# Modulation rows of a two-layer diffusion backbone: turned by VectorE and folded by one matmul, gate row by rounded parts, one section's row sums on VectorE

## The chip, the core and the metric

The kernel runs on one core of a Trainium2 chip. The core has a matmul engine (TensorE, PE in the profile, with its weight loads shown apart as PEld), VectorE (DVE), ScalarE (ACT), GpSimd (POOL) and SyncE (SP), which here only issues DMA transfers. Each engine works through its own list of instructions in order and waits on semaphores for the others. The metric is device time in microseconds (us); several runs are given by their median.

## What is computed

Two transformer layers over 512 latent tokens and 256 context tokens of width 1024. Layer 0 mixes tokens by differential attention (8 heads), layer 1 by grouped-query attention. What the change touches is the adaptive normalisation: for each layer a conditioning vector is multiplied with a 1024 x 3072 matrix, once for the latent tokens (`c`) and once for the context (`c_ctx`), and the result is cut into shift, scale and gate.

```python
def adaln(cvec, w, b):
    m = jax.nn.silu(cvec) @ w + b
    return jnp.split(m, 3, axis=-1)
...
for i in range(DEPTH):
    last = i == DEPTH - 1
    shift, scale, gate = adaln(c, ada_w[i], ada_b[i])
    ...
    cshift, cscale, cgate = adaln(c_ctx, ada_w[i], ada_b[i])
    h = rms_norm(x, pre_g[i]) * (1.0 + scale) + shift
    hc = rms_norm(xc, pre_g[i]) * (1.0 + cscale) + cshift
    ...
    x = x + gate * rms_norm(y, post_g[i])
    if not last:
        xc = xc + cgate * rms_norm(yc, post_g[i])
return x
```

## The kernel before

All matmuls that must be exact to fp32 are made of three fp32r matmuls: each operand is split into a rounded part (`hi`, a ScalarE cast) and the rest (`lo`, a subtraction on GpSimd or VectorE), and hi·hi, hi·lo and lo·hi are summed in PSUM. A plain fp32 matmul is possible too.

**The order of the work.** The program is first recorded as a list of operations by a planner (`Plan`), which prices every operation, keeps track of data, of buffer rings and of PSUM banks, and draws an order for each engine in several passes; `Emit.chain` then fixes that order on every engine. All instructions therefore carry one line number in the profile (L452, the recorder's `add`), and they are told apart by the names of their tiles. Any change of the recorded operations makes the planner draw every engine's order anew.

**The stages.** At the start the tokens are normalised and turned, and layer 0's shift and scale are computed from 32-row blocks (`cols4`, `ada_red`). Then layer 0's heads 0 to 7 run: for each, projections of q, k, v and the gate path z, scores (`sc`), a softmax on VectorE and ScalarE into `pp`, a turn of `pp` (a 32 x 32 block transpose on VectorE, a write to DRAM as `dr`, a reload as `at`), a split of `at` into `ah` and `al`, and the products with v. PSUM has four banks `bk0` to `bk3` and two double banks `sc`. Then come the output projection, the norms of layer 1 and layer 1's heads.

**The modulation in the background.** While layer 0's heads run, the rest of the modulation is computed piece by piece (`acc_steps`). It has six sections of 512 columns, in the order `SECS`: (0,4) and (0,5) are the two halves of layer 0's gate, (1,0), (1,2), (1,1), (1,3) are layer 1's shift and scale. Each section is two groups of four weight blocks; `grp_load` brings a group by one DMA of 1 MB into the single buffer `araw`, `grp_mm` multiplies it, and the next group's load follows.

In `grp_mm` each of the four blocks j goes to its own 32 rows of one PSUM bank. The stationary operand is `s32[:, k, :]`, 32 columns of which the first two hold silu(c) and silu(c_ctx) for block k and the rest are zero. So row 32j+v of the bank holds the part of block j for vector v. The first group is copied to `arow` by ScalarE, the second is added by VectorE. A section listed in `SUMS` would go another way: VectorE multiplies each weight block with the silu column and adds it up, in one `arow` tile for each vector. `SUMS` is empty.

What remains is to add the four blocks over the partitions:

- `ada1_finish` (layer 1's shift and scale) needs the result in columns, one value for each partition. It runs four fp32 matmuls with a 128 x 128 piece of `arow` as weights and `sel32` (128 x 2, ones at rows 32j+v) as the moving operand; `mod_cols` then adds the bias.
- `gate0_finish` (layer 0's gate) needs the row on all partitions. For each of the two vectors it runs one fp32 matmul whose weight is a column of `sel32` broadcast to 128 columns and whose moving operand is all 512 columns of `arow`. VectorE then adds the bias and multiplies.

`ones` and `ones_r` are 128 x 128 tiles of ones, used to warm PE up and to add over partitions (`colsum`).

Of the kernel before, what the change touches and what calls it, by code (L numbers as in the profile page):

```python
# [8 lines left out]
F32 = mybir.dt.float32  # L9
# [6 lines left out]
P = 128  # L16
# [17 lines left out]
ACD = 5.0  # L34
SUMS = ()
FILL1 = (('z', 0), ('q', 2), ('q', 1), ('z', 2), ('z', 1), ('q', 3), ('z', 3), ('z', 4), ('z', 5), ('z', 7), ('z', 6))
# [53 lines left out]
def f32(ap):  # L90
    return ap.bitcast(F32)
# [447 lines left out]
def tile_backbone(  # L539
# [23 lines left out]
    def nm(s):  # L563
        uid[0] += 1
        return f"{s}_{uid[0]}"
# [83 lines left out]
    def heads_out(dst, o, moved):  # L649
# [7 lines left out]
        out=ident, in_=ident, compare_op=ALU.not_equal, fill=1.0, base=0, pattern=[[-1, P]], channel_multiplier=1)  # L657
    ones = con.tile([P, P], F32, name="ones")
    nc.vector.memset(ones, 1.0)
    ones_r = con.tile([P, P], F32R, name="ones_r")  # L660
    nc.vector.tensor_copy(ones_r, ones)
    eps = con.tile([P, 1], F32, name="eps")
# [305 lines left out]
    cp = pool_c.enter_context(pl.pool("cp", "right"))  # L968
    s32 = cp.tile([P, KT, 32], F32, name="s32", bufs=1)
    nc.vector.memset(s32, 0.0)  # L970
    nc.vector.tensor_copy(s32[:, :, 0:2], scv)
    sel32 = cp.tile([P, 2], F32, name="sel32", bufs=1)
    nc.vector.tensor_reduce(sel32, ident.rearrange("p (j r) -> p r j", j=4)[:, 0:2, :], AX.X, ALU.add)
    selb = [sel32[:, v:v + 1].to_broadcast([P, P]) for v in range(2)]

# [3 lines left out]
    def cols4(o, g, ts):  # L979
        prev = None  # L980
        for j in (3, 2, 1, 0):
            with after(prev):
                prev = nc.tensor.matmul(
                    o[32 * j:32 * j + 32, :], s32[:, 4 * g + j, :], ts[j], start=g == 0, stop=g == 1)

# [242 lines left out]
    with pl.pool("t0") as t0:  # L1228
# [11 lines left out]
        def grp_mm(i):  # L1240
# [13 lines left out]
            else:  # L1254
                o = trp()
                prev = None
                for j in range(4):
                    with after(prev):
                        prev = nc.tensor.matmul(o[32 * j:32 * j + 32, :], s32[:, 4 * g + j, :], t[:, j, :], start=True, stop=True)
                r, = rows[layer, sec]  # L1260
# [6 lines left out]
        def ada1_finish(layer, sec):  # L1267
            r = rows.pop((layer, sec))
            o = trp()
            if (layer, sec) in SUMS:  # L1270
                for b in range(8):
                    v, k = divmod(b, 4)
                    nc.tensor.matmul(o[:, b:b + 1], r[v][:, k * P:(k + 1) * P], ones[:, :1], start=b == 0, stop=b == 7)
                ov_ = o[:, :8].rearrange("p (v k) -> p v k", v=2)
            else:
                for b in range(4):
                    nc.tensor.matmul(o[:, 2 * b:2 * b + 2], r[0][:, b * P:(b + 1) * P], sel32, start=b == 0, stop=b == 3)
                ov_ = o[:, :8].rearrange("p (k v) -> p v k", v=2)
            mod_cols(layer, sec % 2, sec // 2, lambda v: ov_[:, v, :])
# [293 lines left out]
        def gate0_finish(half):  # L1573
            r = rows.pop((0, 4 + half))
            sl = slice(half * 512, half * 512 + 512)
            b = bcast(ada_b[0, 2 * D + half * 512:2 * D + half * 512 + 512])
            g = bcast(post_g[0, sl])
            for v in range(2):
                o = trp()
                nc.tensor.matmul(o, *((ones, r[v]) if (0, 4 + half) in SUMS else (selb[v], r[0])), start=True, stop=True)  # L1580
                nc.vector.tensor_tensor(gate0[v][:, sl], o, b, ALU.add)
                nc.vector.tensor_tensor(gate0[v][:, sl], gate0[v][:, sl], g, ALU.mult)
# [712 lines left out]
```

## Time and profile before

| what | value |
| --- | --- |
| median of 3 runs | 764.67 us (764.32 to 766.8) |
| the profiled execution | 763.36 us |
| its span, first to last instruction | 761.6 us |
| instructions | 14035 |
| mean granted clock of the matmul engine | 0.995 |
| data moved by DMA | 131.77 MB, 173 GB/s in the mean |

The busy times of the engines, the stages and the waits are quoted in the prediction. In the profile a line names engine, operation and tiles (result, arrow, operands), the number of instructions, busy time or mean duration, and behind it the idle time of that engine just before and what ended it. A plain fp32 matmul shows as two records, an fp32r matmul as one. The end of a matmul is modelled, so the step from one start to the next tells what it costs PE, not its duration.

### The profile page before, as it was taken

Reading aid. Unit: us, or ns where it says so; the run is one execution under the profiler, and the core shown is the slowest. Engines: PE = TensorE matmul, PEld = TensorE weight load, DVE = VectorE, ACT = ScalarE, POOL = GpSimd, SP = SyncE. Lnnn points to the kernel's source line nnn. Section 1 sums busy time; section 2 is a strip of 40 time slices with the busy share of each in tenths; the row PEclk is TensorE's granted clock in tenths of the full one; section 3 lists DMA queues with packets and bytes.
Section 4 is the critical chain, followed back from the end, with each engine's and each line's share of the span. In section 5 each row is a group of like instructions: output and inputs, shape, how many; then the busy total and the mean of one; then the engine's idle time right before and its main releaser. Section 6 shows DMA issues by size and latency. Waiting matters only on the chain. (4 is left out here: it accounts for less than half of the span.)

```text
span 761.6 us, 14035 instructions
## 1 busy us (share of the span) xinstructions
PE 741.4 (97%) x5070; PEld 657.9 (86%) x5070; DVE 543.5 (71%) x861; ACT 478.7 (63%) x1083; POOL 468.8 (62%) x512
## 2 busy tenths in 40 slices
PE   7999999999999999999999999999999998999996
PEld 6779788888887898888989998899999988987986
DVE  3425789898977778666977843788546887888844
ACT  5534567776566755656748943785356786769641
POOL 3465687986785876747952311476788868774301
PEclk9999999999999999999999999999999999999999
DMA  9961264646576566835667252024537687788713
GB/s 304 363 222 64 95 192 136 184 170 177 168 204 183 185 179 190 248 99 178 196 194 207 106 200 83 2 90 115 167 108 206 198 233 222 223 232 243 211 33 111
DMA packets 69622, 131.77 MB, mean 173 GB/s; under 512 B 6705, under 2 KB 41777, under 8 KB 69553
## 3 DMA queue, kind: packets, MB, share of 16 engines
q1 hardware_dynamic: 66128, 125.73, 54.6%
q10 hardware_dynamic: 3424, 5.15, 2.1%
q8 instruction: 40, 0.66, 0.4%
q14 instruction: 30, 0.24, 0.1%
HBM read 97.56 MB, written 29.10 MB: 166 GB/s over the span
## 5 line engine op out<-in xcount | busy, mean ns | idle before, releaser
L452 PE MATMUL bk<-whi,h 128*128 128x256 f32 (+1 forms) x1184 | 244.7, 300 | 3.6 <-DVE tb L452 1.2
L452 PE MATMUL bk<-h,whi 128*128 128x512 f32 (+2 forms) x832 | 224.8, 349 | 0.1
L452 PEld LDWEIGHTS bk<-whi,h 128*128 128x128 f32 x1184 | 191.5, 190 | 15.9 <-issue 3.3
L452 POOL TENSOR_TENSOR wlo<-raw,whi 128x256 fp32r<-128x256 f32 x200 | 170.5, 876 | 55.9 <-ACT whi L452 48.6
L452 PE MATMUL bk<-wlo,h 128*128 128x256 f32 (+1 forms) x592 | 176.4, 299 | 0.0
L452 PEld LDWEIGHTS bk<-h,whi 128*128 128x128 f32 x832 | 144.4, 188 | 17.2 <-issue 4.7
L452 PE MATMUL bk<-h,wlo 128*128 128x512 f32 (+2 forms) x416 | 144.7, 348 | 0.0
L452 POOL TENSOR_SCALAR pp<-pp,sm 128x768 f32<-128x768 f32 (+1 forms) x78 | 85.2, 1095 | 61.2 <-DVE sm L452 52.7
L452 PEld LDWEIGHTS bk<-wlo,h 128*128 128x128 f32 x592 | 111.9, 189 | 5.0 <-issue 1.5
L452 DVE TENSOR_TENSOR al<-at,ah 128x512 fp32r<-128x512 f32 x103 | 91.8, 908 | 30.6 <-ACT ah L452 25.2
L452 DVE TENSOR_REDUCE sm<-sc 128x1 f32<-128x768 f32 (+2 forms) x114 | 101.0, 893 | 12.6 <-PE sc L452 12.6
L452 ACT CAST whi<-raw 128x1024 fp32r<-128x1024 f32 (+1 forms) x70 | 71.4, 1023 | 23.2 <-PE bk L452 15.7
L452 PEld LDWEIGHTS bk<-h,wlo 128*128 128x128 f32 x416 | 78.3, 188 | 8.1 <-issue 2.1
L452 ACT CAST ah<-at 128x512 fp32r<-128x512 f32 x103 | 61.9, 618 | 34.5 <-PE bk L452 23.7
L452 DVE STREAM_TRANSPOSE pp<-pp 128x1536 f32<-128x1536 f32 (+1 forms) x39 | 61.5, 1578 | 6.5 <-POOL pp L452 6.5
L452 DVE SCALAR_TENSOR_TENSOR pp<-p,sm,pp 128x768 f32<-128x768 f32 (+1 forms) x46 | 55.2, 1207 | 5.3 <-POOL pp L452 4.0
L452 POOL TENSOR_TENSOR sz<-sz,za 128x384 f32<-128x384 f32 (+1 forms) x24 | 31.1, 1295 | 39.1 <-ACT za L452 34.2
L452 PE MATMUL sc<-qk,qk 64*128 64x384 f32 (+1 forms) x480 | 50.7, 341 | 0.5 <-DVE qk L452 0.4
L452 ACT ACTIVATE jk<-bk 128x128 f32<-128x128 f32 (+4 forms) x66 | 22.7, 344 | 42.7 <-PE bk L452 22.9
L452 PEld LDWEIGHTS sc<-qk,qk 64*128 64x128 f32 x480 | 38.2, 184 | 11.6 <-issue 3.6
L452 ACT ACTIVATE pp<-sc,sm 128x768 f32<-128x768 f32 (+1 forms) x46 | 35.5, 772 | 19.7 <-DVE sm L452 19.5
L452 ACT ACTIVATE za<-za 128x384 f32<-128x384 f32 (+1 forms) x72 | 39.7, 558 | 7.4 <-DVE za L452 6.8
(197 smaller groups left out, 1349.8 us busy)
## 6 DMA issues: line engine op xcount, KB each, us to landing
dr<-pp SPq DMA_DIRECT2D x32, 768.0 KB, 3.5
at<-dr SPq DMA_DIRECT2D x128, 192.0 KB, 4.2
raw<-in_a_w SPq DMA_DIRECT2D x30, 512.0 KB, 3.9
araw<-in_ada_w SPq DMA_DIRECT2D x12, 1024.0 KB, 5.8
raw<-in_b_w SPq DMA_DIRECT2D x20, 512.0 KB, 3.6
ag<-in_ada_w SPq DMA_DIRECT2D x32, 256.0 KB, 6.4
raw<-in_w_out SPq DMA_DIRECT2D x16, 512.0 KB, 5.0
sw<-qr ACTq DMA_DIRECT2D x32, 128.0 KB, 2.6
```

What stands on the lines that cost most here:

```text
L452: self.ops.append(getattr(eng, meth)(*args, **kw))
```

## The change

1. **Gate row by rounded parts.** `gate0_finish` splits the `arow` tile into a rounded part (`hi`, ScalarE) and the rest (`lo`, VectorE), both fp32r tiles of the ring `tmp` (three buffers, shared with the rope swap `sw`, the gate path's `za` and the norm's `sqs`; named `rs` in the order). Each fp32 matmul becomes two fp32r matmuls with the broadcast column of `selr`, an fp32r copy of `sel32`.
2. **Turned and folded.** In `ada1_finish` VectorE transposes `arow` in 32 x 32 blocks in place. Row 32j+c of block b then holds in its first two columns the parts of block j for the two vectors at column 32b+c. One fp32 matmul with `fold` (128 x 128, ones where both indices agree modulo 32) adds over j and repeats the result in all four quarters of the partitions; a product with `quad` (128 x 4, ones in the own quarter) and a reduction over it pick, on VectorE, what belongs to each partition.
3. **One section on VectorE.** `SUMS` holds (1,3): its two groups take the existing way of `grp_mm` by VectorE, and its finish is eight fp32 matmuls with a column of ones.
4. **Packed.** `ones` and `ones_r` are one column, broadcast where a 128 x 128 operand is needed. `s32` is 48 columns wide instead of 8 x 32: the silu pairs lie side by side and a weight of 32 columns starts at the pair wanted, so the other 30 rows of a block hold products that nothing reads.

```diff
-SUMS = ()
+SUMS = ((1, 3),)
...
-    ones = con.tile([P, P], F32, name="ones")
-    nc.vector.memset(ones, 1.0)
-    ones_r = con.tile([P, P], F32R, name="ones_r")
-    nc.vector.tensor_copy(ones_r, ones)
+    one = con.tile([P, 1], F32, name="one")
+    nc.vector.memset(one, 1.0)
+    one_r = con.tile([P, 1], F32R, name="one_r")
+    nc.vector.tensor_copy(one_r, one)
+    ones, ones_r = one.to_broadcast([P, P]), one_r.to_broadcast([P, P])
...
-    s32 = cp.tile([P, KT, 32], F32, name="s32", bufs=1)
+    s32 = cp.tile([P, 2 * KT + 32], F32, name="s32", bufs=1)
     nc.vector.memset(s32, 0.0)
-    nc.vector.tensor_copy(s32[:, :, 0:2], scv)
+    nc.vector.tensor_copy(s32[:, 0:2 * KT].rearrange("p (k v) -> p k v", v=2), scv)
...
-    selb = [sel32[:, v:v + 1].to_broadcast([P, P]) for v in range(2)]
+    selr = cp.tile([P, 2], F32R, name="selr", bufs=1)
+    nc.vector.tensor_copy(selr, sel32)
+    selb = [selr[:, v:v + 1].to_broadcast([P, P]) for v in range(2)]
+
+    fold = cp.tile([P, 4, 32], F32, name="fold", bufs=1)
+    for q in range(4):
+        nc.vector.tensor_reduce(fold[:, q], ident.rearrange("p (q c) -> p c q", q=4), AX.X, ALU.add)
+    quad = cp.tile([P, 4], F32, name="quad", bufs=1)
+    nc.vector.tensor_reduce(quad, ident.rearrange("p (q c) -> p q c", q=4), AX.X, ALU.add)
...
-                        prev = nc.tensor.matmul(o[32 * j:32 * j + 32, :], s32[:, 4 * g + j, :], t[:, j, :], start=True, stop=True)
+                        prev = nc.tensor.matmul(o[32 * j:32 * j + 32, :], s32[:, 8 * g + 2 * j:8 * g + 2 * j + 32], t[:, j, :], start=True, stop=True)
...
             if (layer, sec) in SUMS:
                 for b in range(8):
                     v, k = divmod(b, 4)
-                    nc.tensor.matmul(o[:, b:b + 1], r[v][:, k * P:(k + 1) * P], ones[:, :1], start=b == 0, stop=b == 7)
+                    nc.tensor.matmul(o[:, b:b + 1], r[v][:, k * P:(k + 1) * P], one, start=b == 0, stop=b == 7)
                 ov_ = o[:, :8].rearrange("p (v k) -> p v k", v=2)
             else:
-                for b in range(4):
-                    nc.tensor.matmul(o[:, 2 * b:2 * b + 2], r[0][:, b * P:(b + 1) * P], sel32, start=b == 0, stop=b == 3)
-                ov_ = o[:, :8].rearrange("p (k v) -> p v k", v=2)
+                r, = r
+                nc.vector.transpose(r, r)
+                nc.tensor.matmul(
+                    o[:, :32], fold.rearrange("p q c -> p (q c)"),
+                    r.rearrange("p (b x) -> p b x", x=32)[:, :, 0:2], start=True, stop=True)
+                fo = t0.tile([P, 2, 4, 4], F32, tag="fo", name=nm("fo"), bufs=1)
+                nc.vector.tensor_tensor(
+                    fo, o[:, :32].rearrange("p (k q v) -> p v k q", k=4, q=4),
+                    quad.rearrange("p (a b q) -> p a b q", a=1, b=1).to_broadcast([P, 2, 4, 4]), ALU.mult)
+                fc = t0.tile([P, 2, 4], F32, tag="fc", name=nm("fc"), bufs=1)
+                nc.vector.tensor_reduce(fc, fo, AX.X, ALU.add)
+                ov_ = fc
...
         def gate0_finish(half):
-            r = rows.pop((0, 4 + half))
+            r, = rows.pop((0, 4 + half))
+            hi, lo = (t0.tile([P, 512], F32R, tag="tmp", name=nm("rs"), bufs=3) for _ in range(2))
+            nc.scalar.copy(hi, r)
+            nc.vector.tensor_tensor(lo, r, f32(hi), ALU.subtract)
...
-                nc.tensor.matmul(o, *((ones, r[v]) if (0, 4 + half) in SUMS else (selb[v], r[0])), start=True, stop=True)
+                nc.tensor.matmul(o, selb[v], hi, start=True, stop=False)
+                nc.tensor.matmul(o, selb[v], lo, start=False, stop=True)
```

The planner draws the order anew. Three places matter to the prediction. The first is PE at the gate half (0,4), while the value products of layer 0's head 2 run. Before (`vhi`, `vlo` with `ah`, `al` are value products, `whi`, `wlo` with `h` projections):

```order
L452 MATMUL bk1_71<-al_314_2293,vhi_279_1983 128x256 x2
L452 MATMUL bk0_70<-arow_263_1877,sel32_137 128x512
L452 MATMUL bk3_73<-arow_263_1877,sel32_137 128x512
L452 MATMUL bk2_72<-h_42_304,whi_289_2183 128x512
L452 MATMUL bk2_72<-h_43_305,whi_289_2183 128x512
L452 MATMUL bk2_72<-h_42_304,wlo_290_2184 128x512
L452 MATMUL bk1_71<-ah_317_2336,vhi_279_1983 128x256 x2
```

And now:

```order
L452 MATMUL bk1_71<-al_314_2302,vhi_279_1992 128x256 x2
L452 MATMUL bk0_70<-rs_323_2372,selr_139 128x512
L452 MATMUL bk0_70<-rs_324_2373,selr_139 128x512
L452 MATMUL bk3_73<-rs_323_2372,selr_139 128x512
L452 MATMUL bk3_73<-rs_324_2373,selr_139 128x512
L452 MATMUL bk2_72<-h_42_313,whi_289_2192 128x512
L452 MATMUL bk2_72<-h_43_314,whi_289_2192 128x512
L452 MATMUL bk2_72<-h_42_313,wlo_290_2193 128x512
L452 MATMUL bk1_71<-ah_317_2345,vhi_279_1992 128x256 x2
```

Two fp32 matmuls became four fp32r matmuls at the same place between the same neighbours.

The second is VectorE in layer 0's head 6, where the probabilities of its second half (`pp_577` before, `pp_585` now) are finished and turned. Before:

```order
L452 TENSOR_TENSOR al_612_4534<-at_566_4075,ah_611_4533 128x512
L452 SCALAR_TENSOR_TENSOR pp_577_4149<-p_585_4204,sm_582_4184,pp_577_4149 128x24x32
L452 TENSOR_TENSOR sm_614_4550<-sm_614_4550,nlam_122 128x2
L452 STREAM_TRANSPOSE pp_577_4149<-pp_577_4149 128x1536
L452 TENSOR_TENSOR mods_123<-bk2_72,abT_110 128x4 x2
```

And now (`araw_589` is the first group of section (1,3), `arow_611` and `arow_610` are its sums for the two vectors):

```order
L452 TENSOR_TENSOR al_623_4577<-at_574_4100,ah_622_4576 128x512
L452 TENSOR_SCALAR arow_611_4456<-araw_589_4207,scol_114 128x512
...
L452 SCALAR_TENSOR_TENSOR arow_610_4455<-araw_589_4207,scol_114,arow_610_4455 128x512
L452 SCALAR_TENSOR_TENSOR pp_585_4174<-p_593_4229,sm_590_4209,pp_585_4174 128x24x32
L452 TENSOR_REDUCE sm_647_4722<-sc0_74 128x1
L452 TENSOR_TENSOR vlo_609_4367<-bk0_70,vhi_608_4366 128x256
L452 TENSOR_REDUCE sm_648_4727<-sc1_75 128x1
L452 RECIPROCAL sm_645_4708<-sm_645_4708 128x1
L452 SCALAR_TENSOR_TENSOR arow_610_4455<-araw_589_4207,scol_114,arow_610_4455 128x512
L452 STREAM_TRANSPOSE pp_585_4174<-pp_585_4174 128x1536
```

Between the same split and the turn, VectorE now has all eight operations on the first group; the second group's eight follow among head 7's softmax.

The third is the transfer queue SP at the load of the second (1,3) group (`araw_601` before, `araw_612` now), with the spill of that `pp` (`dr`, then `at`). Before:

```order
L452 DMA araw_581_4182<-in_ada_w 128x4x512
L452 DMA dr_587_4211<-pp_577_4149 128x1536
L452 DMA at_586_4210<-dr_587_4211 32x4x384 x4
L452 DMA raw_602_4505<-in_a_w 128x1024
L452 DMA dr_620_4570<-pp_616_4553 128x512
L452 DMA raw_605_4514<-in_w_out 128x4x256
L452 DMA araw_601_4434<-in_ada_w 128x4x512
L452 DMA at_619_4569<-dr_620_4570 32x4x128 x4
```

And now:

```order
L452 DMA araw_589_4207<-in_ada_w 128x4x512
L452 DMA raw_605_4356<-in_a_w 128x1024
L452 DMA raw_613_4536<-in_a_w 128x1024
L452 DMA raw_616_4545<-in_w_out 128x4x256
L452 DMA araw_612_4465<-in_ada_w 128x4x512
L452 DMA dr_595_4236<-pp_585_4174 128x1536
L452 DMA at_594_4235<-dr_595_4236 32x4x384 x4
L452 DMA dr_631_4613<-pp_627_4596 128x512
```

The load of the second group now stands ahead of the spill of head 6's second half; since `araw` is a single buffer, it waits for the eight operations on the first group.

More of the change, by code (lines that the diff above doesn't have):

```diff
@@ L983, in cols4 @@
                 prev = nc.tensor.matmul(
-                    o[32 * j:32 * j + 32, :], s32[:, 4 * g + j, :], ts[j], start=g == 0, stop=g == 1)
+                    o[32 * j:32 * j + 32, :], s32[:, 8 * g + 2 * j:8 * g + 2 * j + 32], ts[j], start=g == 0, stop=g == 1)
     ada_v = ada_w[0].rearrange("(k p) (w n) -> p k w n", p=P, w=3)
```

## The prediction

> **What bounds the kernel now.** I read the page's busy times first, then the table of stages, then the waits of the matmul engine.
>
> ```profile
> PE 741.4 (97%) x5070; PEld 657.9 (86%) x5070; DVE 543.5 (71%) x861; ACT 478.7 (63%) x1083; POOL 468.8 (62%) x512
> ```
>
> A mean of 97% could hide stages with another limit, so the same figures by stage (columns: stage, its length, then busy us of PE, PEld, DVE, ACT, POOL, the granted clock, DMA share, GB/s):
>
> ```profile
> 60.00:372.00 312.00, 310.93 (x2118) 267.48 (x2117) 242.62 (x351) 200.73 (x425) 227.62 (x208) 1.00 0.56 168
> 372.00:390.00 18.00, 18.00 (x149) 15.86 (x149) 15.21 (x26) 9.57 (x20) 14.97 (x15) 1.00 0.76 233
> 390.00:408.00 18.00, 18.00 (x138) 15.94 (x137) 14.74 (x27) 10.93 (x23) 5.87 (x7) 1.00 0.61 178
> 408.00:447.00 39.00, 39.00 (x297) 38.72 (x297) 27.19 (x41) 31.94 (x66) 12.36 (x10) 1.00 0.46 151
> 480.00:600.00 120.00, 118.88 (x863) 112.34 (x862) 83.84 (x167) 76.52 (x223) 88.53 (x118) 1.00 0.42 125
> 600.00:640.00 40.00, 35.88 (x232) 33.17 (x231) 32.49 (x46) 28.79 (x66) 29.95 (x31) 0.96 0.80 236
> 640.00:720.00 80.00, 78.54 (x486) 70.96 (x486) 68.42 (x94) 63.05 (x132) 46.61 (x44) 1.00 0.80 223
> ```
>
> From 60 to 447 us PE is idle for 1.07 us in 387. The modulation work of `grp_mm`, `ada1_finish` and `gate0_finish` lies between 158 and 404 us, inside that stretch. There a matmul taken off PE shortens the program by its own time, as long as nothing that feeds PE gets later. Later PE does wait: 4.12 us between 600 and 640, 1.46 between 640 and 720. For what, say the waits of PE from 600 to 745 us (in total, times, longest):
>
> ```profile
> PE bk L452 <- DVE tb L452: 1.2, 1, 1.2
> PE bk L452 <- DVE al L452: 1.2, 1, 1.2
> PE bk L452 <- ACT g L452: 0.9, 2, 0.5
> PE bk L452 <- ACT sz L452: 0.7, 1, 0.7
> ```
>
> These are layer 1's hand-overs from VectorE and ScalarE. Nothing of the change runs there, though its instruction order is drawn anew.
>
> **Gate rows (0,4) and (0,5).** What PE does around the first one:
>
> ```profile
> 206.39 1.88 PE L452 MATMUL bk<-arow,sel 128*128 128x512 f32 x4
> 207.70 1.03 PE L452 MATMUL bk<-h,whi 128*128 128x512 f32 x2
> 208.57 0.39 PE L452 MATMUL bk<-h,wlo 128*128 128x512 f32 x1
> 208.80 0.40 PE L452 MATMUL bk<-ah,vhi 128*128 128x256 f32 x2
> ```
>
> The fp32r matmul at 208.57 is followed 0.23 us later by the next, so 0.23 is a 512-column fp32r step. From 206.39 to 208.57, 2.18 us, lie four records of the two fp32 gate matmuls and two fp32r steps: 2.18 - 0.46 = 1.72, 0.43 a record, 0.86 a matmul. Afterwards each half has four fp32r matmuls, 4 x 0.23 = 0.92, so 0.80 is saved per half, **1.6 for both**. Does an fp32r matmul on a one-column broadcast weight pay once? The records say how many passes each kind makes (minimum, median, maximum ns; first and last start):
>
> ```profile
> L452 PE MATMUL bk<-arow,sel x8: 592/592/592, 206.4 to 246.5; 128*128 128x512 f32 x8
> ```
> ```profile
> L452 PE MATMUL bk<-sqs,ones_r x32: 282/338/444, 129.3 to 441.1; 128*128 128x384 f32 x28, 128*128 128x512 f32 x2, 128*128 128x256 f32 x2
> ```
>
> Four fp32 calls left eight records; the 32 fp32r calls of the norm's column sums left 32. The gate weight is a broadcast column already and its records run at the fp32 pace, so broadcasting costs nothing visible. The worst case is therefore a pass at 0.43 each, a gain of 0 here; I take 1.6.
>
> The chain in front grows: the addition into `arow`, then ScalarE's cast and VectorE's subtraction of the rest (about 0.6 and 0.7 us). The first of the six additions is that of (0,4):
>
> ```profile
> L452 DVE TENSOR_TENSOR arow<-bk,arow x6: 646/684/692, 183.2 to 397.8; 128x512 f32<-128x512 f32 x6
> ```
>
> 183.2, and PE reads the row at 206.39: 23 us cover 1.3. Without that cover PE would wait the 1.3, with the value products queued behind the gate in the order above.
>
> **Folding (1,0), (1,2), (1,1).** The finish of a section now:
>
> ```profile
> 299.26 0.95 PE L452 MATMUL bk<-sel,arow 128*128 128x2 f32 x8
> 300.06 0.48 PE L452 MATMUL bk<-ah,vhi 128*128 128x256 f32 x2
> ```
>
> Four fp32 matmuls of two columns, eight records in 0.80 us, 0.10 each: the weight, not the columns, sets that. One fp32 matmul of 32 columns is two records, 0.20 us; if 32 columns cost as much as a 512-column record it would be 0.86. Nearest is the two-column row. 0.60 saved each, **1.8 for three** (bounds -0.2 and 1.8).
>
> **Row sums of (1,3) on VectorE.** One of its two groups on PE:
>
> ```profile
> 385.00 1.06 PE L452 MATMUL bk<-araw,s 128*32 128x512 f32 x8
> 386.00 0.39 PE L452 MATMUL bk<-whi,h 128*128 128x256 f32 x1
> ```
>
> 1.00 us a group, 2.0 for both, go. Its finish grows from four to eight fp32 matmuls, of one column: 16 records at 0.10, 1.6 where 0.8 stood. Net **1.2** (0.4 to 2.0, if a one-column record costs 0.15 or 0.05). PE's sum is 1.6 + 1.8 + 1.2 = **4.6 us**.
>
> **What VectorE takes on.** Prices:
>
> ```profile
> L452 DVE SCALAR_TENSOR_TENSOR gacc<-gw,scol,gacc x14: 735/822/1772, 513.2 to 544.1; 128x512 f32<-128x512 f32 x14
> ...
> L452 DVE TENSOR_SCALAR gacc<-gw,scol x2: 469/490/510, 512.3 to 532.5; 128x512 f32<-128x512 f32 x2
> ```
> ```profile
> L452 DVE STREAM_TRANSPOSE pp<-pp 128x512 f32<-128x512 f32 x7 | 4.9, 700 | 0.0
> L452 DVE TENSOR_TENSOR arow<-bk,arow 128x512 f32<-128x512 f32 x6 | 4.1, 677 | 6.6 <-PE bk L452 6.6
> L452 DVE TENSOR_REDUCE ls<-lm 128x2 f32<-128x128 f32 x1 | 0.3, 277 | 0.0
> ```
>
> The `gacc` rows are the same operation in the same shape: 14 x 0.82 + 2 x 0.49 - 0.68 (one `arow` addition less) = 11.8 us more for (1,3). Each folded section adds a turn of 0.70 and two small operations, about 1.0; each gate half a subtraction of about 0.7. The gates and (1,0), (1,2) fall before 372, where DVE is busy 242.6 of 312 and PE has 1.07 us of idle time: hidden. ScalarE gets two casts and loses one copy: nothing. The weight is in 372 to 447, where (1,1) ends and all of (1,3) runs: DVE is busy there 15.2 + 14.7 + 27.2 = 57.1 of 75 us, so 17.9 are free; with PE 4.6 shorter, 13.3. The additions there are 11.8 + 1.0 = 12.8. It fits, with half a microsecond to spare, so some hand-over to PE will come late. I price that by half of the one `al` wait quoted above, **0.6 us**.
>
> Where it would show: the two sets of four one-column matmuls are new waits of PE for VectorE. Behind the first stand head 6's value products and a score unit, behind the second the gate projection (`z`) of head 7, all in PE's order and so all held with it; what VectorE itself holds behind the sums is head 7's turns and the splits of its probabilities (`al`).
>
> At the start five strided reductions of the identity (0.28 each by the `ls` row, 1.4 us) and a cast fall into a hole of DVE:
>
> ```profile
> 6.44 0.17 DVE L452 SCALAR_TENSOR_TENSOR preb<-abT,pre 128x8 f32<-128x8 f32 x1 [4.95 <-DMA abT<-in_ada_bT]
> ```
>
> 4.95 us idle: free; without the hole 1.4.
>
> **Queue.** Behind the second (1,3) load SP now holds the spill of head 6's second half (in the order above). That load waits for eight sums. The turn that the spill needs and the first reading of its reloaded tile stood at:
>
> ```profile
> 371.27 1.77 DVE L452 STREAM_TRANSPOSE pp<-pp 128x1536 f32<-128x1536 f32 x1
> ...
> 403.87 0.69 DVE L452 TENSOR_TENSOR al<-at,ah 128x512 fp32r<-128x512 f32 x1 [0.42 <-ACT ah L452]
> ```
>
> 32.6 us apart. The turn now comes after eight sums (7 us) and some ten other rows, roughly 12 us later, so the tile still comes in time: 0. The two slots of the three-deep `tmp` ring that a gate half holds delay rope or gate tiles by a DVE row or two: 0 on PE.
>
> **Sum.** 4.6 - 0.6 = 4.0 us. The profiled execution took 763.36 with a span of 761.6; 763.36 - 4.0 = 759.4. The median of the three runs, 764.67, lies 1.3 above the profiled one: **760.7**.
>
> **Rivals.**
> *VectorE against GpSimd (slower).* The `gacc` row runs from 0.735 to 1.772 us for one shape, and GpSimd's subtraction doubles too:
>
> ```profile
> L452 POOL TENSOR_TENSOR wlo<-raw,whi x200: 723/746/1482, 17.5 to 671.6; 128x256 fp32r<-128x256 f32 x100
> ```
>
> If every sum met such an operation, 14 x (1.77 - 0.82) = 13.3 us more would stand on DVE where 0.5 is free: the last sums, and behind them the transposes of head 7, would hold PE some 12 us, 760.7 + 12 = 773; with half of them, 767. It decides from about 7 us of added contention. For it: POOL is busy 15.0 of 18 us from 372 to 390. Against it: only 5.9 of 18 and 12.4 of 39 after that, when the second group's eight sums run, and the median is 0.82. The Trainium skill, SBUF — State Buffer, section "Who interferes with whom", has this as a rule: a VectorE instruction with two SBUF inputs contends with a GpSimd instruction that reads SBUF, and whoever comes second blocks. By that rule the time comes out between 760.7 and 773, by the share of sums that meet one; the trace's doubled rows agree with it.
> *Late loads (no change).* If the second (1,3) load waits 20 us longer than I take, head 6's and head 7's reloads are late and PE loses about the 4 us it gained: 764.7.
> *Layer 1 drawn worse (no change).* PE's 5.6 us of waits between 600 and 720 depend on the order of heads and projections, drawn anew; half as much again takes back 2.8: 763.5. Twice as much: 766.3.
> *No fewer passes.* fp32r on the broadcast column at 0.43: 1.6 of the gain gone, 762.3.
>
> **Chances.** Forecast 0.57, own range 758.5 to 762.4. Passes 0.05 (still faster). Late loads 0.08 and layer 1 worse 0.15, nearly all within 0.3%, which is about what a measurement of this kernel can tell from no change: 762.4 to 767.0. Contention 0.15, slower. Faster 0.62, same 0.23, slower 0.15. For 8 in 10 the range goes from 757.0 (all of the 4.6, and 2 of layer 1's waits gone with it) to 767.0 (half the sums contended).
>
> **What would show it.** Right: PE's busy time down by 4 to 5 us, two records less than 0.3 us together per folded section, gate halves at about 0.95 us, PE at 39 of 39 us before layer 0's last projection. Wrong: PE waiting for `arow` or `al` between 365 and 445 us, sums above 1.2 us on average, or PE waits in layer 1 well off 5.6 us.

## The result and the profile after

The change made the kernel slower: 767.17 us in the median of 19 runs (764.87 to 770.14) against 764.32 (762.35 to 766.8) for the kernel before in the same session, a ratio of 1.004, 95% interval 1.003 to 1.005. The profiled execution took 766.15 us with a span of 764.4.

The busy times of the whole span, first part of the page of the changed kernel:

```profile
PE 740.6 (97%) x5044; PEld 658.3 (86%) x5044; DVE 569.5 (75%) x893; ACT 479.5 (63%) x1084; POOL 469.0 (61%) x512
```

VectorE took on 26 us (543.5 before). PE shows 0.8 us less. The stages of the changed kernel (stage, length, busy us of PE, PEld, DVE, ACT, POOL, granted clock, DMA share, GB/s):

```profile
60.00:369.00 309.00, 306.30 (x2087) 264.14 (x2086) 248.37 (x358) 200.41 (x426) 220.54 (x205) 1.00 0.55 169
369.00:387.00 18.00, 17.15 (x143) 16.30 (x142) 18.00 (x25) 8.11 (x17) 14.00 (x12) 1.00 0.40 124
387.00:405.00 18.00, 18.00 (x136) 16.84 (x135) 17.34 (x29) 10.96 (x24) 11.76 (x10) 1.00 0.55 169
405.00:444.00 39.00, 36.53 (x264) 34.61 (x264) 33.61 (x54) 30.80 (x67) 14.89 (x11) 1.00 0.52 162
```

Before, PE was idle for 1.07 us in the first stage and not at all in the next three; now it is idle for 2.70 us in the first, 0.85 in the second and 2.47 in the last. VectorE is busy in 18.00 of 18 us from 369 and in 17.34 of 18 from 387. What PE waits for between 60 and 600 us (in total, times, longest):

```profile
PE bk L452 <- DMA araw<-in_ada_w: 1.9, 1, 1.9
PE bk L452 <- DVE al L452: 1.5, 2, 1.3
PE bk L452 <- DVE kl L452: 1.3, 1, 1.3
PE sc L452 <- ACT p L452: 0.9, 1, 0.9
PE bk L452 <- ACT gT L452: 0.8, 1, 0.8
```

Before, PE waited in the same stretch for 0.3 us for `araw`, for 0.5 us for `kl`, and not for the others. New or longer are a weight load at 229 us (`araw`, 1.9), a softmax at 382 (`p`, 0.9), the output of a head at 409 (`gT`, 0.8), the split of head 7's probabilities at 431 (`al`, 1.3) and, in layer 1, `kl`. The row sums themselves, by tile:

```profile
L452 DVE SCALAR_TENSOR_TENSOR arow<-araw,scol,arow x14: 740/1138/2330, 369.6 to 411.4; 128x512 f32<-128x512 f32 x14
```

Median 1.14 us where the same operation in the same shape had 0.82 in layer 1; the fourteen take 16.6 us.

The matmul steps came out as priced. Starts of PE's instructions, at the first fold and at the second set of column sums:

```profile
299.59 0.30 PE L452 MATMUL bk<-arow,fold 128*128 128x32 f32 x2
299.73 0.48 PE L452 MATMUL bk<-ah,vhi 128*128 128x256 f32 x2
```
```profile
413.46 0.95 PE L452 MATMUL bk<-one,arow 128*128 128x1 f32 x8
414.27 0.42 PE L452 MATMUL bk<-h,whi 128*128 128x384 f32 x1
```

A fold costs 299.73 - 299.59 = 0.14 us in place of 0.81, a set of four one-column matmuls 0.81. A gate half has four fp32r matmuls in 0.93 us (205.96 to 206.89). So PE was given 2 x 0.8 + 3 x 0.67 + (2.0 - 0.81) = 4.8 us less. Its busy time shows only 0.8 of that. Busy time is no pure count of work: the kernel before and its three variants with the same matmuls (below) show 740.1 to 744.5 us of it. A part of the missing 4.0 us is the clock, 0.993 granted instead of 0.995, by estimate 1.5 us of 764; where the rest is, is not shown. The question is why the time went the other way.

### The profile page after: what moved, and what is told of

It is laid out like the page before. It is cut to its first block, busy times and chain, and to the rows that moved or that the text cites. A ratio compares the mean times of both kernels' runs of the same rounds, so it can differ in the third digit from the quotient of the medians.

```text
span 764.4 us, 14010 instructions
## 1 busy us (share of the span) xinstructions
PE 740.6 (97%) x5044; PEld 658.3 (86%) x5044; DVE 569.5 (75%) x893; ACT 479.5 (63%) x1084; POOL 469.0 (61%) x512
## 4 chain that ended last, share of the span: by engine, by line
PE 72%; DVE 9%; DMA 8%; ACT 4%; issue 4%; SPq 2%; POOL 1%; DVEq 0%; ACTq 0%; POOLq 0%
PE bk L452 60%; PE sc L452 12%; DMA at<-dr 3%; DVE al L452 2%; DMA dr<-pp 2%; SPq L452 2%; DVE h L452 1%; DVE arow L452 1%; DMA araw<-in_ada_w 1%; DVE sm L452 1%; DMA xt<-in_x 1%; DMA raw<-in_a_w 1%; ACT whi L452 1%; ACT ah L452 1%; DVE pp L452 1%
## 5 line engine op out<-in xcount | busy, mean ns | idle before, releaser
L452 PEld LDWEIGHTS bk<-h,whi 128*128 128x128 f32 x832 | 144.4, 188 | 17.9 <-issue 3.7
L452 POOL TENSOR_SCALAR pp<-pp,sm 128x768 f32<-128x768 f32 (+1 forms) x78 | 82.1, 1054 | 53.7 <-DVE sm L452 44.1
L452 DVE TENSOR_TENSOR al<-at,ah 128x512 fp32r<-128x512 f32 x103 | 100.0, 992 | 15.9 <-ACT ah L452 12.8
L452 POOL TENSOR_TENSOR sz<-sz,za 128x384 f32<-128x384 f32 (+1 forms) x24 | 29.4, 1225 | 36.6 <-ACT za L452 30.4
```

Of the source, the lines that this page charges most:

```text
L452: self.ops.append(getattr(eng, meth)(*args, **kw))
```

## The experiments

Each comparison is with runs of the kernel before on the same chip. The medians of the kernel before on the five chips used lie between 763.6 and 764.3 us, and the versions are compared by their ratios to it; 0.001 is 0.76 us. The version without row sums is the change with `SUMS` empty, all four sections of layer 1 folded.

| kernel | us, median | ratio | 95% interval |
| --- | --- | --- | --- |
| the change | 767.17 | 1.0040 | 1.003 to 1.005 |
| no row sums | 761.36 | 0.9977 | 0.9956 to 0.9998 |
| the change, sums thin, order held | 765.57 | 1.0025 | 1.0013 to 1.0037 |
| no row sums, gates in fp32, order held | 766.19 | 1.0044 | 1.0026 to 1.0061 |
| before, packing alone | 762.85 | 0.9987 | 0.9969 to 1.0005 |
| before, DPAD 780 | 766.95 | 1.0049 | 1.003 to 1.0068 |
| before, MARGIN 1.09 | 769.23 | 1.0068 | 1.0043 to 1.0093 |
| no row sums, DPAD 780 | 763.34 | 0.9993 | 0.9979 to 1.0008 |
| no row sums, MARGIN 1.09 | 764.90 | 1.0004 | 0.9984 to 1.0023 |
| the change, DPAD 780 | 769.60 | 1.0094 | 1.0064 to 1.0125 |
| packing and sums alone | 765.77 | 1.0043 | 1.0023 to 1.0064 |
| sums for (1,0) instead | 764.67 | 1.0018 | 0.9999 to 1.0038 |
| sums for (1,2) instead | 766.81 | 1.0049 | 1.0029 to 1.0068 |
| sums, planner told 32 columns | 769.90 | 1.0082 | 1.0056 to 1.0108 |
| gate alone | 770.21 | 1.0082 | 1.0049 to 1.0114 |
| fold alone | 770.98 | 1.0091 | 1.0063 to 1.0119 |
| gate and packing | 767.75 | 1.0056 | 1.0039 to 1.0074 |
| fold and packing | 766.11 | 1.0035 | 1.0019 to 1.0051 |
| no row sums, slower load price | 772.02 | 1.0106 | 1.0084 to 1.0128 |

Two theories were tested. **Theory 1**: the sums fill VectorE, and PE waits for what stands behind them. **Theory 2**: the order that the planner drew anew costs the time, whatever the sums take.

### One part out, one part alone

```diff
-SUMS = ((1, 3),)
+SUMS = ()
```

> The change with SUMS empty again: (1,3) goes the folded way like the other three sections. PE loses the two groups' 2.0 us again but the finish is 0.2 instead of 1.6, so PE's own work is 4.0 us less than before the change. Theory 1 (the sums on VectorE cost PE 3 to 4 us of waits between 365 and 445 us): those waits fall under 1 us, and the time is 3 us under that of the change, 763 to 765. Theory 2 (any redrawn order costs 2 to 3 us of waits, the sums are nothing special): 766 to 768, with waits of 3 us in other places. The wait of about 2 us for the load of the second group of (0,5) near 229 us stays by both, since up to about 365 us the order is that of the change.

The other three are made of the kernel before and pieces of the diff above: part 4 with the line of `SUMS`, part 1 alone, and part 2 alone, for all four sections.

> The kernel before with the packed columns and section (1,3) on VectorE alone; gate and the other sections as before. PE's own work falls by 1.2 us. Theory 1: 3 to 4 us of waits of PE between 365 and 445 us, so 2 to 3 us slower than before, 766 to 767. Theory 2: between 764 and 768, with the waits spread over the program.

> The kernel before with the gate row by rounded parts alone. PE's own work falls by 1.6 us. Theory 1: 762.5 to 763.5, no new wait above 1 us. Theory 2: 764 to 767. A third theory, that the two extra slots of the ring of temporary tiles and the late subtraction (2.3 us in one of the two cases) hold back PE: the wait for the load near 229 us is there too, 765 to 766.

> The kernel before with all four sections of layer 1 turned and folded, the gate as before, SUMS empty. PE's own work falls by 4 x 0.6 = 2.4 us. Theory 1: 761.5 to 763. Theory 2: 764 to 767.

Without the sums the kernel is faster than before, 0.9977, though the interval nearly reaches 1. Up to about 365 us its order is that of the change; layer 1 (the first turn of `gate` on PE) begins at 500.4 us instead of 506.8 (504.8 before). PE's idle time from 350 to 450 us falls to 0.5 us, as theory 1 had it, and the time fell further than it expected. The sums with the packing alone are slower than before, but PE is idle for 1.5 us in that stretch and not for 3 to 4. So far theory 1, in part. But the gate alone and the fold alone are slower by 0.8 and 0.9%, more than any theory expected, although each takes work off PE, and together, with the packing, they are faster. No price of a single piece explains that: theory 2 has its part.

### The order held

The planner's and the emitting pass run the same code, so a size that differs between them changes the work and leaves the order alone. The first edit makes the sums short, the second makes the gates of the version without sums long (in the emitting pass only):

```diff
+n = 512 if isinstance(pl, Plan) else 32
-nc.vector.scalar_tensor_tensor(r, t[:, j, :], s, r, ALU.mult, ALU.add)
+nc.vector.scalar_tensor_tensor(r[:, :n], t[:, j, :n], s, r[:, :n], ALU.mult, ALU.add)
```
```diff
-nc.tensor.matmul(o, selb[v], hi, start=True, stop=False)
-nc.tensor.matmul(o, selb[v], lo, start=False, stop=True)
+nc.tensor.matmul(o, self32[v], f32(hi), start=True, stop=False)
+nc.tensor.matmul(o, self32[v], f32(lo), start=False, stop=True)
```

> The change with its order held on every engine, row for row: the planner records the row sums of section (1,3) at their full 512 columns and draws the same order, but the 14 additions on VectorE work on 32 columns only (the two first products stay at 512). Left out: what blocks 1 to 7 add to the sums of (1,3) on columns 32 to 511. About 14 x 1.0 = 14 us of VectorE go away between 369 and 415 us, nothing else. Theory 1, the sums hold VectorE up and VectorE holds PE up: the 5 to 6 us come back, about 762 (ratio 0.997 to 0.999), and the waits of PE and its idle 2.5 us between 405 and 444 us are gone. Theory 2, the newly drawn order as such (who stands behind whom, whatever the sums take) costs the time: it stays at 766 to 767 (ratio 1.003 to 1.005). A value between, 764 to 765, would share the loss between the two.

> The order of the version without row sums on VectorE held row for row (761.4 us), with the eight fp32r matmuls of the gate rows made as plain fp32 matmuls of the same operands: 8 x (0.86 - 0.23) = 5.0 us more of work on PE, between 200 and 250 us, nothing else moved. If PE sets the time there and the order is held, as the prediction assumed for the work that the change takes off it: 761.4 + 5.0 = 766.4 (ratio about 1.004). If the 1.6 us wait of PE for the araw load at 228 us takes up a part (the load is late by that much, whatever PE does ahead of it): 3.4 us, 764.8. If PE is not what sets the time in that stretch: under 763.

The first gate half of the long version, starts on PE:

```profile
205.87 3.60 PE L452 MATMUL bk<-rs,sel 128*128 128x512 f32 x8
208.90 1.02 PE L452 MATMUL bk<-h,whi 128*128 128x512 f32 x2
209.76 0.39 PE L452 MATMUL bk<-h,wlo 128*128 128x512 f32 x1
```

From 205.87 to 209.76 lie eight fp32 records and two fp32r steps of 0.23: 3.43 us, 2.50 more than 0.93. Twice that is 5.0, and the ratio rose by 0.0067, 5.1 us, with some 2 us to either side, since both ratios have their interval. In the profiled executions layer 1 began 3.2 us later (503.6), and the 1.4 us wait for `araw` at 228 was gone; together that is 4.6. **With the order held, PE's work went into the time within this accuracy**, less a wait that it covers: the prediction's first assumption stands.

The thin sums fell by only 0.0015, 1.1 us, from the change, which the two intervals do not tell from nothing, and stand 3.7 us above the version without sums. From 350 to 450 us, the kernel before, the change, the thin sums and the version without sums, one row each:

```profile
350.00:450.00 100.00, 100.00 (x747) 92.50 (x746) 75.27 (x120) 69.23 (x149) 54.20 (x48) 1.00 0.61 188
```
```profile
350.00:450.00 100.00, 96.68 (x708) 89.93 (x707) 85.95 (x134) 66.18 (x140) 57.67 (x48) 1.00 0.56 176
```
```profile
350.00:450.00 100.00, 97.53 (x711) 91.18 (x709) 77.58 (x132) 65.29 (x141) 51.54 (x47) 0.98 0.56 176
```
```profile
350.00:450.00 100.00, 99.49 (x745) 91.99 (x745) 76.94 (x125) 68.38 (x154) 52.09 (x52) 1.00 0.60 192
```

With thin sums VectorE has as little to do as without sums (77.58 against 76.94), and PE still loses 2.47 us where the other loses 0.51. So the length of the sums is not most of what PE waits for in this order: the wait for `p` at 382 us is gone, those for `gT` (0.8) and `al` (1.3) stay. What they come from is seen at the end of layer 0. VectorE's rows of the change, with the version without sums behind:

```profile
413.69 0.68 DVE L452 TENSOR_TENSOR al<-at,ah 128x512 fp32r<-128x512 f32 x1
...
417.17 1.83 DVE L452 TENSOR_TENSOR h<-gT,h 128x768 fp32r<-128x768 f32 x2 [0.53 <-ACT h L452]
...
421.75 2.11 DVE L452 TENSOR_TENSOR al<-at,ah 128x512 fp32r<-128x512 f32 x2
...
424.65 0.68 DVE L452 TENSOR_TENSOR al<-at,ah 128x512 fp32r<-128x512 f32 x1
...
428.31 3.52 DVE L452 TENSOR_TENSOR al<-at,ah 128x512 fp32r<-128x512 f32 x3
```
```profile
410.23 0.68 DVE L452 TENSOR_TENSOR al<-at,ah 128x512 fp32r<-128x512 f32 x1
...
412.74 1.16 DVE L452 TENSOR_TENSOR al<-at,ah 128x512 fp32r<-128x512 f32 x1 [0.92 <-ACT ah L452]
...
414.29 0.88 DVE L452 TENSOR_TENSOR al<-at,ah 128x512 fp32r<-128x512 f32 x1
...
416.01 1.11 DVE L452 TENSOR_TENSOR al<-at,ah 128x512 fp32r<-128x512 f32 x1 [0.45 <-ACT ah L452]
...
417.66 1.16 DVE L452 TENSOR_TENSOR h<-gT,h 128x768 fp32r<-128x768 f32 x1
```

Without sums four splits of probabilities stand ahead of the first `h` (the head outputs' rest). In the change one of these does, and six stand behind `h` rows, which wait for head 7's gate projection; the last of head 7's scores start at 412.1 us instead of 406.5 (406.2 before). The thin kernel has the same rows, and VectorE idle in front of them:

```profile
414.41 1.83 DVE L452 TENSOR_TENSOR h<-gT,h 128x768 fp32r<-128x768 f32 x2 [1.78 <-ACT h L452]
```

The wait is 1.78 us instead of 0.53: VectorE's freed time turned into idle time. The chain of work that ended last (start, us, link) agrees. In the change four of the operations on the sums are a link of it, and from 416.3 to 431.8 us it goes through `h` and `al`, down to the split that PE waits for at 431:

```profile
370.89 6.06 DVE arow L452 x4
...
431.16 0.68 DVE al L452
```

In the thin kernel that link of `arow` is gone, and those of `h` and `al` are still there. Without sums the chain stays on PE at that place, with this as its longest link:

```profile
407.08 14.57 PE bk L452 x93
```

### What a draw is worth

```diff
-DPAD = 800
+DPAD = 780
```

```diff
-MARGIN = 1.08
+MARGIN = 1.09
```

The packing alone is part 4 of the change.

> The kernel before with the packed ones and silu columns alone: no matmul is added, removed or made longer on any engine, only sizes of two tiles change, and with them the planner's placing and drawing. If the pieces of the change act by the work they add and remove: 763.6 as before, within 0.3%. If the drawn order by itself moves the time by several us (theory 2): off by more than 2 us in either direction, and the difference of 2.2 us between the packed version with the sums and the kernel before says then little about the sums.

> The kernel before with one planner constant (DPAD) at 780 instead of 800: the same operations with the same sizes, another order. It measures what an order drawn anew is worth with no other change. Theory 2 expects 765 to 771, as for the gate alone and the fold alone (the kernel before was drawn by the best of many constants, so another draw is likely worse); if the draw were harmless, 763.6 within 0.3%, and the slowness of the gate alone (770.2) and of the fold alone (771.0) would have to come from their own instructions.

> The kernel before with another planner constant (MARGIN 1.09 instead of 1.08), nothing else. A third draw of the kernel before, beside 764.0 and 767.0: anywhere in 762 to 768 if draws are worth about 2 us either way.

> The whole change, drawn with the same other constant (DPAD 780) that took the kernel before from 764.1 to 767.0. If the row sums themselves make the change slow, it stays at 766 or above, as 767.2 with the constant of the change. If the change saves its PE work and loses it only in the order that happened to be drawn (theory 2), this draw can fall on either side of 764.1, and set against the kernel before under the same constant (767.0) it should be lower by something like the 3 to 5 us of PE work: 762 to 764.

> The version without row sums on VectorE (761.4), drawn with DPAD 780. Theory 2: PE's saved work of about 3.4 us stands against the kernel before under the same constant (767.0), so 763 to 764, and the spread between draws of one kernel is about 3 us. If 761.4 came from the parts alone and the draw did nothing there: 761.4 again.

> The version without row sums (gate by rounded parts, four folds, packing) under the same MARGIN 1.09. In the two pairs with equal constants it stood 2.6 (764.0 to 761.4) and 3.7 (767.0 to 763.3) below the kernel before; its PE work is 1.6 + 4 x 0.67 = 4.3 us less. If that work passes through in the mean over draws: 2 to 5 us below the other run of this pair. If the two pairs were luck of the draw: the difference may have either sign.

The packing is no draw of its own. Its trace shows the order of the kernel before on every engine, row for row by the tiles' names, and the same holds for the gate, and for the fold, with the packing (below) and without. Each of these three pairs is one order measured twice, gate and fold on two chips, and the ratios differ by 0.0013, 0.0026 and 0.0056. Whether the packed tiles or the measurement do that is not shown; in the last pair the granted clock was 0.992 and 0.997 in the median. A difference of that size between two rows of the table decides little by itself.

Three draws of the same matmuls stand at 1, 1.0049 and 1.0068: a range of 0.7%, 5 us, with no matmul added or removed. That is more than the whole gain looked for. Under equal constants the comparison is steadier. Without sums against before: -0.0023, -0.0056 and -0.0064, in the mean -0.0048 or 3.6 us, where PE has 2 x 0.8 + 4 x 0.67 = 4.3 less. The intervals of the three are 0.002 to 0.003 to each side; all three have one sign, and the first and the last are each from one chip. The sums against their own version without sums: +0.0063 (the change), +0.0101 (DPAD 780, on one chip), and for the packing with sums +0.0056 against the packing alone, +0.0043 against the kernel before: 3 to 8 us of loss.

### The sums elsewhere, and unannounced

```diff
-SUMS = ((1, 3),)
+SUMS = ((1, 0),)
```
```diff
+n = 32 if isinstance(pl, Plan) else 512
-nc.vector.scalar_tensor_tensor(r, t[:, j, :], s, r, ALU.mult, ALU.add)
+nc.vector.scalar_tensor_tensor(r[:, :n], t[:, j, :n], s, r[:, :n], ALU.mult, ALU.add)
```

The version for (1,2) is written like the first.

> The whole change with the row sums on VectorE for section (1,0), which runs between about 250 and 300 us in the middle of layer 0, in place of (1,3) at the end of the layer; the other sections are folded. PE's own work is the same as in the change. If the loss of the sums (2.9, 5.8 and 6.3 us in three pairs of draws) comes from their place, the last 60 us of layer 0 in which VectorE is full and nothing is left to put in front of a late softmax: 761 to 763. If VectorE has no room for 14 such operations anywhere in layer 0: 765 to 768, with the idle time of PE between 250 and 330 us. A draw as such is worth about 2 us either way.

> The same with section (1,2), between about 300 and 330 us. Place: 761 to 763; no room anywhere: 765 to 768, with the idle time of PE between 300 and 370 us. With the version for (1,0) it makes two draws of each answer.

> The whole change, nothing left out, but the planner is told that the 14 additions have 32 columns, about 14 x 1 us less on VectorE than they take. So it draws as if the sums cost next to nothing there, and the sums then take what they take. If the planner's making room for the sums at the end of layer 0 is what costs (theory 2): about 761 to 763, if the draw is no worse elsewhere. If VectorE has no room for the sums (theory 1, the step of the prediction with half a microsecond to spare): 766 to 769, with PE waiting for al, h or pp between 370 and 445 us by some 10 us, since nobody made room for them.

The stage 250 to 350 us of the first two, (1,0) and (1,2), and 350 to 450 of the third:

```profile
250.00:350.00 100.00, 96.51 (x666) 84.92 (x668) 79.22 (x120) 60.62 (x132) 69.84 (x65) 1.00 0.58 174
```
```profile
250.00:350.00 100.00, 97.78 (x661) 87.25 (x658) 87.92 (x121) 60.34 (x128) 69.85 (x65) 0.97 0.59 179
```
```profile
350.00:450.00 100.00, 94.51 (x678) 88.23 (x677) 87.84 (x127) 65.79 (x139) 57.27 (x48) 0.97 0.53 163
```

The idle time of PE follows the sums: 3.5 and 2.2 us where they now stand, and 0.1 and 0.0 from 350 to 450. Idle us of PE by stage, length less busy time:

| kernel | 160 to 250 | 250 to 350 | 350 to 450 | 450 to 600 |
| --- | --- | --- | --- | --- |
| before; packing alone | 0.2; 0.2 | 0.3; 0.0 | 0.0; 0.0 | 1.1; 1.1 |
| before, DPAD 780; MARGIN 1.09 | 0.0; 1.7 | 0.1; 1.4 | 2.2; 0.2 | 1.2; 1.4 |
| no sums; its two redraws | 1.5; 0.8; 0.9 | 0.0; 0.7; 0.0 | 0.5; 0.4; 0.6 | 0.9; 1.9; 2.3 |
| sums (1,3): change; DPAD 780; packing only | 2.0; 0.4; 0.3 | 0.0; 1.1; 0.0 | 3.3; 4.3; 1.5 | 1.7; 1.8; 2.6 |
| sums (1,3), planner told 32 columns | 2.0 | 0.3 | 5.5 | 0.9 |
| sums (1,0); (1,2) | 2.0; 0.6 | 3.5; 2.2 | 0.1; 0.0 | 0.5; 2.2 |
| gate and packing; fold and packing | 3.9; 2.4 | 0.9; 0.7 | 0.6; 0.2 | 1.6; 2.2 |
| gate alone; fold alone | 2.3; 2.4 | 1.0; 0.0 | 1.2; 0.2 | 2.1; 2.2 |
| no sums, slower load price | 3.4 | 2.6 | 0.7 | 1.3 |

In six versions PE is idle for 1.5 to 5.5 us in the stage of the sums. Of the twelve versions without them, two have more than 0.7 from 350 to 450 (2.2 and 1.2); from 250 to 350, though, one has 2.6, more than (1,2) with its sums. None of the three places was free: (1,0), (1,2) and (1,3) stand 0.0041, 0.0072 and 0.0063 over no sums, which the intervals hardly tell apart. In time (1,2) fell into the range expected for no room anywhere, (1,0) between the two ranges. That VectorE has no room for fourteen such operations anywhere in layer 0 is suggested by this, not shown. Unannounced, the sums hold the softmax:

```profile
PE sc L452 <- ACT p L452: 5.0, 2, 3.3
```

That is theory 1 in its pure form, with waits of 5.0 us, half of what was expected of it, and a ratio 0.0105 above no sums. Announced, the planner makes room, and the price, 0.0063, is paid mostly in the order. So the two theories can be read as two forms of one shortage; this is argued and not shown, since the unannounced version is another draw too.

### Gate and fold with the packing, and a truer load price

Parts 1 and 4 together, parts 2 and 4 together, and one entry in the planner's table of DMA prices:

```diff
-rate, base = {196608: (207, 1450), 786432: (420, 900), 131072: (350, 2500)}.get(op.cost, (350, 1450))
+rate, base = {196608: (207, 1450), 786432: (420, 900), 131072: (350, 2500), 1048576: (200, 1450)}.get(op.cost, (350, 1450))
```

The rate before was the default of 350, not the 250 that the expectation names.

> The packing and the gate rows by rounded parts, no fold, no sums. The gate alone without the packing took 770.2, the packing alone 762.9. If a piece is worth its PE work and the draw is worth about 2 us either way: 762.9 - 1.6 = 761.3, between 759 and 764. If the gate's own new instructions (cast, subtraction, two slots of the tmp ring) cost 6 us as the version without the packing would say: 767 to 769.

> The packing and all four sections folded, gate as before, no sums. The fold alone without the packing took 771.0. If a piece is worth its PE work: 762.9 - 4 x 0.67 = 760.2, between 758 and 763. If the turn of arow and the two small operations cost what the version without the packing would say: 768 to 770.

> The version without row sums, with the planner's rate for the 1 MB weight loads changed from 250 to 200 bytes a nanosecond and a fixed part of 1.45 us, so that it plans their landing some 6.7 us after the issue, as the traces show in a busy stretch (6.0 to 7.9). If the 1.4 to 1.9 us wait of PE for araw at 228 us is a cost that a truer price removes: 759.5 to 760, the best of all. If the draw decides instead: anywhere in 760 to 767, with that wait gone or not.

Both single parts stayed slower, by 0.0069 and 0.0048 over the packing alone: the absence of the packing was not the reason. The time of the gate is the one expected if its own instructions cost it (767 to 769). Their idle time lies between 160 and 250 us, the stage of the gate. The waits of PE from 160 to 260 us, gate with packing, then fold with packing:

```profile
PE sc L452 <- ACT p L452: 1.6, 1, 1.6
PE bk L452 <- DMA araw<-in_ada_w: 1.0, 1, 1.0
PE bk L452 <- DVE rs L452: 0.7, 1, 0.7
PE bk L452 <- POOL sqs L452: 0.6, 1, 0.6
PE bk L452 <- DVE gate L452: 0.5, 1, 0.5
```
```profile
PE bk L452 <- DMA araw<-in_ada_w: 2.1, 1, 2.1
```

The gate's own subtraction (`rs`) accounts for 0.7 us and its result for 0.5; the 0.6 for the norm's `sqs` may be due to the ring `tmp`, which both use. The fold's first turn of `arow` comes later (283.3 us), and it waits 2.1 us there all the same. So a good part of it is order, but how much isn't shown for either. The truer price for the load drew the slowest kernel of all, 1.0106: the wait for `araw` that it aimed at, 1.4 us, is gone, but between 160 and 350 us PE is now idle for 6.0 us instead of 1.5. The best version is the one without row sums, 0.9977, within the spread of draws.

## Why the prediction was wrong, point by point

The forecast was 760.7 us, 4.0 below the kernel before; measured were 767.17, 2.85 above it in the same session.

- **PE bounds the kernel, and its work passes through.** Right within some 2 us: 5.0 us of added PE work cost 5.1 with the order held. The sign named for it, PE's busy time down by 4 to 5 us, did not come: it fell by 0.8.
- **Gate 1.6, fold 1.8, (1,3) 1.2.** Right in size: 0.93 us a gate half, 0.14 a fold, 0.81 a set of column sums. Yet 1.2 was the wrong comparison for the section: against folding it as well, the sums save only 2.0 + 0.14 - 1.62 = 0.5 us of PE, for 16.6 us of VectorE.
- **"It fits, with half a microsecond to spare", and 0.6 us for the late hand-over.** This is the step that failed, with its sum of free time over 372 to 447. The sums stand between 369 and 412 us. There VectorE had 18 - 15.21 and 18 - 14.74, some 6 us free, by the rows of the prediction. Much of the 17.9 us lay behind, where head 7's softmax is over: from 430 to 450 the kernel before shows VectorE busy for 11.31 of 20 us. And the additions took 16.6 us, with the two first products (0.96 each) and without the dropped `arow` addition 17.9, not 11.8. In place of 0.6 us the runs showed 3 to 8. Free time of an engine is room only where the work can stand; the waits that took its place were `p`, `gT` and `al`, as "what would show it" named for `al`.
- **VectorE against GpSimd.** The rival's 767 is the time that was measured, and its mechanism is in the trace. VectorE and GpSimd at the first group, then one sum in a hole of GpSimd and GpSimd's next row:

```profile
372.16 4.79 DVE L452 SCALAR_TENSOR_TENSOR arow<-araw,scol,arow 128x512 f32<-128x512 f32 x3
```
```profile
372.90 2.19 POOL L452 TENSOR_TENSOR qk<-qr,qk 128x768 fp32r<-128x768 f32 x1
375.07 1.34 POOL L452 TENSOR_SCALAR pp<-pp,sm 128x768 f32<-128x768 f32 x1
```
```profile
408.02 0.74 DVE L452 SCALAR_TENSOR_TENSOR arow<-araw,scol,arow 128x512 f32<-128x512 f32 x1
```
```profile
408.93 1.86 POOL L452 TENSOR_SCALAR pp<-pp,sm 128x768 f32<-128x768 f32 x1 [4.03 <-DVE sm L452]
```

  Alone a sum takes 0.74 us; three beside `qk` and `pp` take 4.79. Of the fourteen, twelve overlap GpSimd for at least half of their length, and 16.6 - 14 x 0.74 = 6.2 us are added. The contention itself was put too low: the median of the `gacc` rows came from a stretch with its own overlap, and the argument against it looked at GpSimd's mean, not at what runs beside the sums. But the time was not lost in the way the rival had it: making the sums short returned 1.1 us, not 6, so that its 767 met the measured time is in good part luck. The Trainium skill, SBUF — State Buffer, section "Who interferes with whom", says that the later of two such instructions blocks until the earlier ends. The trace agrees: each of the twelve began while a GpSimd instruction ran and ended 0.54 to 0.55 us after the end of that one, which gave lengths from 0.89 to 2.33 us.
- **Layer 1 drawn worse.** No: PE's idle time from 600 to 745 us is 5.07 after and 5.58 before.
- **Late loads, queue, start.** The spill and its reload made no wait between 383 and 431 us, as predicted. A load did come late elsewhere: the second group of (0,5). From issue to landing in 218 to 236 us (minimum, median, maximum), the change, then the thin sums, whose order is the same there:

```profile
DMA to landing us min/median/max: 7.0/7.4/7.9
```
```profile
DMA to landing us min/median/max: 6.0/6.4/6.8
```

  The one waits 1.9 us and the other doesn't. The prediction priced the queue only at (1,3); in the kernel before, the weight load ahead of that matmul already waited 0.4 us for it, so it had no slack.
- **The order.** The prediction held three places against each other and took the rest as unchanged. Draws of unchanged work differ by 5 us, so the own range of 4 us around the forecast was too narrow by construction.

Open remain the share of the order and of contention in the 3 to 8 us for each draw, and what makes the gate alone and the fold alone slow. Taking the contention away with the order held was not tried.

## What to carry to other kernels

Room on an engine is counted in the stretch in which the moved work must stand, at the duration it has beside its neighbours there, and against the best alternative for the same work: 16.6 us of VectorE bought 0.5 us of PE. Where a planner redraws the whole order, measure first what a redraw of unchanged work is worth, see in the trace whether the order did change, and judge an edit by pairs under several constants or with the order held. An edit with the order held tells what an operation costs; an edit with the order drawn anew tells what the planner makes of it.

## What was not expected of the hardware

PE can pay for a wait a second time. In the unannounced version the granted clock fell at its longest wait, 3.3 us that ended at 387.9 (columns as above, clock third from the end):

```profile
370.00:390.00 20.00, 16.74 (x132) 15.79 (x131) 19.28 (x28) 9.02 (x18) 15.35 (x14) 0.92 0.76 221
390.00:410.00 20.00, 18.22 (x123) 17.08 (x121) 19.55 (x26) 9.28 (x18) 8.26 (x7) 0.91 0.21 78
386.70:393.50 6.80, 5.64 (x28) 5.20 (x29) 6.78 (x12) 1.25 (x3) 4.22 (x3) 0.50 0.64 191
```

The third row shows what the means of the first two hide: half the clock for 6.8 us, so 3.4 us of full speed are lost beside the 5.0 us of waits. The second wait, 1.8 us that ended at 407.7, had no such effect: the clock is 1.00 from 407 to 430. From which length on a wait does this is not settled: the thin sums show 0.91 from 430 to 450 us behind a wait of 1.3 us, the change 1.00 throughout layer 0, with its waits of 0.8 to 1.9 us.
